# Score products over all 128 rows and two head slots' P·V on both column halves, in a hybrid attention and mixture-of-experts block

## The chip, the cores and the metric

The kernel runs on one core of a Trainium2 chip. Its time is the device time of one execution in microseconds (us). In the listings PE is the tensor engine (matrix products), PEld its loading of the stationary operand, DVE the vector engine, ACT the scalar engine, POOL the general engine, SP the engine whose queue issues nearly all DMA transfers. Engines run side by side, each takes its instructions in their order, and semaphores make one wait for another. SBUF is the on-chip memory with 128 rows (partitions); PSUM holds the products' sums.

## What is computed

One decoder layer over 256 tokens of width 1024, in float32:

```
h = rmsnorm(x);  proj = h @ w_in
y_dil = dilated attention: 3 groups x 8 heads (dilation 1, 4, 16), head width 64;
        the 3 heads of a slot are combined by their softmax denominators
y_swa = sliding-window attention: 16 query heads, 2 key/value heads, with sinks
x += (sigmoid(gate_d) * (y_dil @ w_br_dil) + sigmoid(gate_s) * (y_swa @ w_br_swa)) @ w_out
x += experts: one group of 4, then 2 of its 8 SwiGLU experts per token, width 512
out = rmsnorm(x)
```

All 32 experts' weights are read: each has 6 MB, against 36 MB of dense weights.

## The kernel before

**Stages.** The dense weights come as tiles of 512 columns by 4 row blocks (1 MB, class `Stream`, four slots). `convert` (L232) splits each pair of row blocks on ACT (L248) and DVE (L249) into two float32r parts, high and low. A dense product of two split operands is three matmuls (`three`, L345): high·high, low·high, high·low, each 128x128 by 128x256 or 128x512; they are called `acc` in the trace. The units of 512 columns follow one another: q, k and v of the dilated heads; then k, v, q of the windowed heads and the first gate, with the eight dilated head slots (`dil_slot`, L558) interleaved step by step (L773); then the second gate and the first branch product, interleaved with the eight pairs of windowed heads (`swa_pair`, L521; L780); then the branch and output products, the router, and the 32 experts one after the other (L1061 on).

**Scores.** The score products are split in three as well. For the head of slot i = 2a + b, tile `qa[:, b, a]` holds the high parts of q on 64 rows and its low parts on the other 64, and `ka[:, b, a]` holds the high parts of k on both halves of the rows. So one product over 128 rows gives high·high + low·high (L565). The third, high·low, runs over only the 64 rows with the high parts of q, against `kal`, the low parts of k (L566). Four small float32 products per half of the queries (L570) add the two wider groups. Windowed heads do the same with `kx` and `kxl` (L528, L529), 256 keys for either half of the queries. A plain float32 product shows as two matmul instructions in the trace, a float32r one as one.

**After the scores**, `softmax` (L487) runs on DVE and ACT, PE transposes the probabilities (`dtp` L579, `stp` L542), and P·V follows (`dpv`, `spv`). In `dil_slot` the slot with b = 0 writes the columns of the array that give PSUM rows 0 to 63, the one with b = 1 those of rows 64 to 127, each slot in its own step (L586 to L590). In `swa_pair` both heads' products of one size stand next to each other, on either half of the columns (L546 to L551). The two `pT` buffers of the transposed probabilities are in tile `turnedp` (L519).

**Order and memory.** `pipelined` (L596) takes the scores of one slot, the transposes of the one before and the values of the one before that; `interleave` (L616) puts these steps between those of the dense units at a ratio. The framework's scheduler then fixes each engine's order. SBUF is handed out in numbered slots of 1 MB. Expert weights come in 1 MB pieces (`ew`; two DMAs of 512 KB for gate and up, or one for down) into a ring of such slots. Slots 20 and 23 are in the ring from the start (L639), and two pieces are loaded during the first units (L769 to L771); each `release` (L661) adds slots that have become free and issues one piece for each. The ring's later pieces are issued as an expert's products free their slots.

Of the kernel before, what the change touches and what calls it, by code (L numbers as in the profile page):

```python
# [17 lines left out]
P = 128  # L18
T = 256
# [18 lines left out]
def _constants():  # L38
    """Tables that depend on the shapes alone: distances of the score blocks with the
    masked ones far away, unit and triangular matrices, counters, the scales of q."""  # L40
# [44 lines left out]
def tile_hybrid_block(  # L85
# [24 lines left out]
    # x and the output come with the tokens by their class, the token modulo 4, and in order within it:  # L110
    # place 64 c + j is token 4 j + c.
# [19 lines left out]
    # ---------------------------------------------------------------- loads  # L131
# [22 lines left out]
    class Stream:  # L154
        """Dense weights, 512 columns by 4 row blocks of 128, in the order they are used."""
# [71 lines left out]
    # ---------------------------------------------------------------- splitting of dense weights  # L227
# [4 lines left out]
    def convert(order=lambda i: i):  # L232
        """Split the next two row blocks of a dense weight into two float32r parts, exactly."""
# [35 lines left out]
    # ---------------------------------------------------------------- h = rmsnorm(x), transposed, split  # L269
# [52 lines left out]
    # ---------------------------------------------------------------- dense products  # L322
    # q and k of the widest products in two float32r parts: on one half of the partitions the high parts of
    # a head's q, on the other its low parts; the high parts of k on both; the low parts of k.
    qa = slot(4, [P, 2, 4, T], "qa", F32R)
    ka = slot(22, [P, 2, 4, T], "ka", F32R)
    s21 = slot(21, [P, 2048], "ks", F32R)
    kal = s21[:, 0:1024].rearrange("p (a t) -> p a t", a=4)
    kx, kxl = (s21[:, c:c + 512].rearrange("p (j t) -> p j t", j=2) for c in (1024, 1536))
# [31 lines left out]
    def evac(un, half, o):  # L361
# [41 lines left out]
        elif kind == "kd" and arg == 0:  # L403
            c = slice(2 * half, 2 * half + 2)
            for b in range(2):
                own = slice(64 * b, 64 * b + 64)
                for r in (own, slice(64 - 64 * b, 128 - 64 * b)):
                    A.copy(ka[r, b, c, :], ov[own])
                V.tensor_tensor(out=kal[own, c, :], in0=ov[own], in1=ka[own, b, c, :].bitcast(F32), op=ALU.subtract)
# [11 lines left out]
        elif kind == "brs":  # L421
            if half == 0:
                # the first half of the sum is in two parts before the second half begins, which takes its place
                mixed[arg] = (sb.tile([P, 2, 4, T], F32R, tag="PT", name="mixed0") if arg == 0
                              else slot(0, [P, 2, 4, T], "mixed1", F32R))
# [14 lines left out]
    def unit_steps(u):  # L440
        """One unit as steps of a row-block pair each: two passes over the same weights."""
# [44 lines left out]
    # ---------------------------------------------------------------- attention  # L486
    def softmax(pt_, parts, sinkcols=None):  # L487
        """parts: (scores in PSUM, distances, scale, start of the minimum) -> P and 1/denominator.
        Scores come with the sign turned, so their minimum is minus the maximum."""
# [29 lines left out]
    turnedp = sb.tile([P, 2, 768], F32, tag="PT", name="pT")  # L519

    def swa_pair(a):  # L521
        kv = a // 4
        sc = quad[2 * (a % 2):2 * (a % 2) + 2]
        for b in range(2):
            r = slice(64 * b, 64 * b + 64)
            for t in range(NT):
                q, o = qs[b][:, a, t * P:(t + 1) * P], sc[b][:, T * t:T * t + T]
                mm(o, q, kx[:, kv, :], True, False)  # L528
                mm(o, q[r], kxl[r, kv, :], False, True)  # L529
# [28 lines left out]
    def dil_slot(i):  # L558
        """One head slot of the dilated attention: in the two wider groups a query's keys are of its class."""
# [3 lines left out]
        for h in range(2):  # L563
            q = qa[:, b, a, h * P:(h + 1) * P]
            mm(sc[h][:, 0:T], q, ka[:, b, a, :], True, False)  # L565
            mm(sc[h][:, 0:T], q[r], kal[r, a, :], False, True)  # L566
# [8 lines left out]
        pT = turnedp[:, i % 2, :]  # L575
# [6 lines left out]
        if b == 0:  # L582
            late["dpv"] = bank("V", [P, 512], f"dpv{a}")
        o = late["dpv"]
        hc = slice(64 * i, 64 * i + 64)
        for t in range(NT):  # L586
            mm(o[r, 0:T], vd[t][:, 0, hc], pT[:, T * t:T * t + T], t == 0, False)
        for c in range(4):
            mm(o[r, 64 * c:64 * c + 64], vd[c // 2][:, 1 + c % 2, hc], pT[:, 2 * T + 64 * c:2 * T + 64 * c + 64],
               False, c == 3)  # L590
        if b == 1:
            A.copy(yd[:, 0, a, :], o[:, 0:T])
            V.tensor_tensor(out=yd[:, 1, a, :], in0=o[:, 0:T], in1=yd[:, 0, a, :].bitcast(F32), op=ALU.subtract)
        yield

    def pipelined(gens, parts):  # L596
        """Scores of one, transposes of the one before, values of the one before that."""
# [34 lines left out]
    # ---------------------------------------------------------------- expert weights  # L632
# [6 lines left out]
    ring = [20, 23]  # L639
# [21 lines left out]
    def release(*slots):  # L661
        """These slots are free for expert weights from here on."""
# [14 lines left out]
    # ---------------------------------------------------------------- routing  # L677
# [12 lines left out]
    def route_piece(t, k):  # L690
        """256 columns of x2 of one token tile: squares summed, transposed for the logits."""
# [23 lines left out]
    def route_pick(t):  # L715
        """The first of the best groups, its two best experts, the pairs' places in line."""
# [411 lines left out]
```

## Time and profile before

| | us |
|---|---|
| device time, median of 3 runs (780.91 to 783.07) | 781.64 |
| span of the profiled execution, first to last instruction | 779.8 |
| PE busy in the span | 674.3 |
| DVE busy | 294.6 |
| ACT busy | 225.9 |
| bytes moved by DMA | 249.89 MB |

The execution's own time is not listed apart from its span; the median of the timed runs is 1.84 us above the span. PE is busy in all of the first half and less in the second, where the DMA moves a steady 408 GB/s. A share of busy time over the whole span hides that the stages have different limits, so the stages are read one by one below.

### The profile page before, as it was taken

How to read it: one execution, taken by the hardware profiler on the slowest of the kernel's cores; microseconds unless marked ns; L12 is line 12 of the kernel's file. 1: busy time of each engine (PE TensorE's matmuls, PEld its weight loads, DVE VectorE, ACT ScalarE, POOL GpSimd, SP SyncE). 2: the span in 40 equal slices, each digit the busy share in tenths (PEclk: the TensorE clock that was granted, in tenths of full speed). 3: DMA queues.
4: the chain of work that ended last, by engine and by line, in shares of the span. 5: the costliest groups of instructions: out<-in, count | busy, mean ns of one | idle time of the engine just before them, and what ended most of it. 6: DMA issues, size and time to landing. Idle time of an engine off the chain costs nothing.

```text
span 779.8 us, 15115 instructions
## 1 busy us (share of the span) xinstructions
PE 674.3 (86%) x6417; PEld 478.2 (61%) x6417; DVE 294.6 (38%) x749; ACT 225.9 (29%) x448; POOL 2.1 (0%) x10
## 2 busy tenths in 40 slices
PE   9999999999999999999987777878787787767682
PEld 8998988889788998765645334444434344433341
DVE  6564667874666675632222111211211111111102
ACT  5444575755677454310101000100000000000003
POOL 0000000000000000000000000000000000000000
PEclk9999999999999999999999679888978958987787
DMA  8786554336634778999999999999999999999993
GB/s 310 248 307 207 162 187 139 109 109 254 232 109 156 273 293 311 337 369 407 408 408 410 408 408 408 408 407 408 409 409 408 409 409 409 408 407 409 408 408 135
DMA packets 81054, 249.89 MB, mean 320 GB/s; under 512 B 8652, under 2 KB 10072, under 8 KB 80984
## 3 DMA queue, kind: packets, MB, share of 16 engines
q1 hardware_dynamic: 80824, 248.82, 83.5%
q8 instruction: 52, 0.85, 0.4%
q14 instruction: 18, 0.15, 0.1%
q10 hardware_dynamic: 160, 0.07, 0.0%
HBM read 247.82 MB, written 1.05 MB: 319 GB/s over the span
## 4 chain that ended last, share of the span: by engine, by line
PE 55%; DMA 38%; DVE 3%; ACT 2%; issue 1%; SPq 0%; ACTq 0%; DVEq 0%
PE acc L121 29%; DMA ew<-in_w_e_up_dram 17%; DMA ew<-in_w_e_down_dram 11%; DMA ew<-in_w_e_gate_dram 10%; PE gu L121 7%; PE quad L121 7%; PE dn L121 4%; PE ga L121 3%; PE dpv L121 1%; PE ct L899 1%; PE spv L121 1%; PE dtp L579 1%; PE stp L542 1%; PE ct L121 1%; PE atp L127 1%
## 5 line engine op out<-in xcount | busy, mean ns | idle before, releaser
L121 PE MATMUL gu<-ew,xes 128*32 128x256 f32 x2048 | 153.7, 416 | 36.9 <-DMA ew<-in_w_e_up_dram 36.9
L121 PE MATMUL acc<-hT_hi,wh 128*128 128x256 f32 x800 | 147.7, 285 | 0.8 <-DVE qa L401 0.8
L121 PEld LDWEIGHTS acc<-hT_hi,wh 128*128 128x128 f32 x800 | 122.0, 188 | 4.4 <-issue 1.5
L121 PEld LDWEIGHTS gu<-ew,xes 128*32 128x32 f32 x2048 | 64.9, 116 | 93.8 <-issue 64.0
L249 DVE TENSOR_TENSOR wh<-w,wh 128x1024 fp32r<-128x1024 f32 (+1 forms) x84 | 100.2, 1198 | 44.3 <-ACT wh L248 42.7
L121 PE MATMUL acc<-hT_lo,wh 128*128 128x256 f32 x400 | 111.4, 279 | 0.0
L248 ACT CAST wh<-w 128x1024 fp32r<-128x1024 f32 (+1 forms) x84 | 86.1, 1028 | 49.7 <-PE acc L121 42.9
L121 PE MATMUL dn<-ew,ws 128*32 128x256 f32 x1024 | 84.8, 468 | 3.5 <-DMA ew<-in_w_e_down_dram 2.8
L925 DVE TENSOR_TENSOR ws<-ws,gu 128x128 f32<-128x128 f32 x32 | 9.2, 286 | 194.0 <-ACT ws L922 194.0
L121 PEld LDWEIGHTS acc<-hT_lo,wh 128*128 128x128 f32 x400 | 75.1, 188 | 0.4 <-issue 0.4
L922 ACT ACTIVATE ws<-gu 128x128 f32<-128x128 f32 x32 | 8.9, 278 | 215.1 <-PE gu L121 215.1
L121 PEld LDWEIGHTS dn<-ew,ws 128*32 128x32 f32 x1024 | 33.1, 128 | 33.2 <-issue 12.8
L951 ACT ACTIVATE y_hi<-dn,gsl 128x256 fp32r<-128x256 f32 x32 | 15.2, 474 | 114.5 <-PE dn L121 114.5
L121 PE MATMUL ga<-ws,x_again 128*128 128x128 f32 x256 | 39.3, 315 | 4.8 <-DVE ws L938 3.8
L121 PEld LDWEIGHTS ga<-ws,x_again 128*128 128x128 f32 x256 | 36.0, 221 | 8.9 <-DVE ws L938 6.9
L953 DVE SCALAR_TENSOR_TENSOR y_lo<-dn,gsl,y_hi 128x256 fp32r<-128x256 f32 x32 | 15.5, 483 | 66.6 <-ACT y_hi L951 66.6
L121 PE MATMUL quad<-y_hi,cts 32*128 32x256 f32 x256 | 24.0, 361 | 15.0 <-ACT y_hi L951 15.0
L121 PEld LDWEIGHTS quad<-y_hi,cts 32*128 32x128 f32 x256 | 14.2, 208 | 33.3 <-ACT y_hi L951 32.1
L121 PE MATMUL quad<-y_lo,cts 32*128 32x256 f32 x256 | 32.6, 392 | 2.3
L860 ACT ACTIVATE xes<-ga,fcol 128x128 f32<-128x128 f32 x32 | 11.7, 368 | 79.0 <-DVE xes L862 79.0
L892 DVE TENSOR_SCALAR ws<-cs,pos 128x128 f32<-128x128 f32 x64 | 17.8, 281 | 41.6 <-PE ct L121 41.6
L121 PEld LDWEIGHTS quad<-y_lo,cts 32*128 32x128 f32 x256 | 19.0, 205 | 21.9 <-issue 14.3
(199 smaller groups left out, 769.0 us busy)
## 6 DMA issues: line engine op xcount, KB each, us to landing
ew<-in_w_e_gate_dram SPq DMA_DIRECT2D x128, 512.0 KB, 12.7
ew<-in_w_e_up_dram SPq DMA_DIRECT2D x128, 512.0 KB, 12.8
ew<-in_w_e_down_dram SPq DMA_DIRECT2D x63, 1024.0 KB, 12.7
w<-in_w_in_dram SPq DMA_DIRECT2D x29, 1024.0 KB, 5.2
w<-in_w_br_swa_dram SPq DMA_DIRECT2D x4, 1024.0 KB, 5.2
w<-in_w_out_dram SPq DMA_DIRECT2D x4, 1024.0 KB, 6.6
w<-in_w_in_dram SPq DMA_DIRECT2D x4, 512.0 KB, 5.8
w<-in_w_br_dil_dram SPq DMA_DIRECT2D x2, 1024.0 KB, 5.2
```

Source lines behind the costliest of these rows:

```text
L121: i = PE.matmul(o, lhsT, rhs, start=start, stop=stop, skip_group_check=True)
L127: i = PE.transpose(o, src, ident)
L248: order(A.copy(w[:, 0, :, :ncol], r))
L249: order(V.tensor_tensor(out=w[:, 1, :, :ncol], in0=r, in1=w[:, 0, :, :ncol].bitcast(F32), op=ALU.subtract))
L542: PE.transpose(tp[:, j * P:(j + 1) * P], pp[:, 384 * b + j * P:384 * b + (j + 1) * P], ident)
L579: PE.transpose(tp[:, h * P:(h + 1) * P], pp[:, 384 * h + j * P:384 * h + (j + 1) * P], ident)
L860: A.activation(dst, src, AF.Copy, scale=col)
L892: eq = V.tensor_scalar(dd[:, t, :].rearrange("p (g s) -> p g s", g=REP), cs[:, C_CNT:C_CNT + CAP].unsqueeze(1).to_broadcast([P, REP, CAP]) ...
L922: A.activation(ac, gu[:, 0:P], AF.Silu)
L925: V.tensor_tensor(out=ac, in0=ac, in1=gu[:, P:2 * P], op=ALU.mult)
L951: A.activation(y_hi, dn[:, 0:256], AF.Copy, scale=gsl)
L953: V.scalar_tensor_tensor(out=y_lo, in0=dn[:, 0:256], scalar=gsl, in1=y_hi.bitcast(F32), op0=ALU.mult, op1=ALU.subtract)
```

## The change

It has four parts. (1) `kal` gets a slot of its own and holds the low parts of k on both halves of the rows; the third score product of `dil_slot` and of `swa_pair` uses all 128 rows of q. In the product of q's low half with the low parts of k, low·low is added, which the version before left out. (2) In `dil_slot` the four wide score products come first, then all eight small ones; in `swa_pair` the first half of the queries gets only the 128 keys that it uses. (3) P·V of two dilated slots is done in one step, product by product alternating between the two column halves; `pT` has four buffers, two of them in slot 20. (4) Slots 20 and 23 come into the ring only after the dilated slots, so the two early pieces are no longer loaded ahead; the steps' ratio goes from 40 to 36.

```diff
-    kal = s21[:, 0:1024].rearrange("p (a t) -> p a t", a=4)
-    kx, kxl = (s21[:, c:c + 512].rearrange("p (j t) -> p j t", j=2) for c in (1024, 1536))
+    kal = slot(23, [P, 2, 4, T], "kal", F32R)
+    kx, kxl = (s21[:, c:c + 512].rearrange("p (j t) -> p j t", j=2) for c in (0, 512))
...
-                for r in (own, slice(64 - 64 * b, 128 - 64 * b)):
+                both = (own, slice(64 - 64 * b, 128 - 64 * b))
+                for r in both:
                     A.copy(ka[r, b, c, :], ov[own])
-                V.tensor_tensor(out=kal[own, c, :], in0=ov[own], in1=ka[own, b, c, :].bitcast(F32), op=ALU.subtract)
+                for r in both:
+                    V.tensor_tensor(out=kal[r, b, c, :], in0=ov[own], in1=ka[own, b, c, :].bitcast(F32),
+                                    op=ALU.subtract)
...
     turnedp = sb.tile([P, 2, 768], F32, tag="PT", name="pT")
+    more = slot(20, [P, 2048], "pT2")[:, 0:1536].rearrange("p (i c) -> p i c", i=2)
+    turned4 = [turnedp[:, 0, :], turnedp[:, 1, :], more[:, 0, :], more[:, 1, :]]
...
-                q, o = qs[b][:, a, t * P:(t + 1) * P], sc[b][:, T * t:T * t + T]
-                mm(o, q, kx[:, kv, :], True, False)
-                mm(o, q[r], kxl[r, kv, :], False, True)
+                n = P * (t + 1)
+                q, o = qs[b][:, a, t * P:(t + 1) * P], sc[b][:, T * t:T * t + n]
+                mm(o, q, kx[:, kv, 0:n], True, False)
+                mm(o, q, kxl[:, kv, 0:n], False, True)
...
             mm(sc[h][:, 0:T], q, ka[:, b, a, :], True, False)
-            mm(sc[h][:, 0:T], q[r], kal[r, a, :], False, True)
+            mm(sc[h][:, 0:T], q, kal[:, b, a, :], False, True)
+        for h in range(2):
             for g in (1, 2):
...
-        pT = turnedp[:, i % 2, :]
+        pT = turned4[i % 4]
...
         if b == 0:
-            late["dpv"] = bank("V", [P, 512], f"dpv{a}")
-        o = late["dpv"]
-        hc = slice(64 * i, 64 * i + 64)
+            return
+        o = bank("V", [P, 512], f"dpv{a}")
+        two = [(slice(64 * j, 64 * j + 64), slice(64 * (2 * a + j), 64 * (2 * a + j) + 64), turned4[(2 * a + j) % 4])
+               for j in range(2)]
         for t in range(NT):
-            mm(o[r, 0:T], vd[t][:, 0, hc], pT[:, T * t:T * t + T], t == 0, False)
+            for r, hc, pT in two:
+                mm(o[r, 0:T], vd[t][:, 0, hc], pT[:, T * t:T * t + T], t == 0, False)
         for c in range(4):
-            mm(o[r, 64 * c:64 * c + 64], vd[c // 2][:, 1 + c % 2, hc], pT[:, 2 * T + 64 * c:2 * T + 64 * c + 64],
-               False, c == 3)
...
+            cl = slice(64 * c, 64 * c + 64)
+            for r, hc, pT in two:
+                mm(o[r, cl], vd[c // 2][:, 1 + c % 2, hc], pT[:, 2 * T + 64 * c:2 * T + 64 * c + 64], False, c == 3)
...
-    ring = [20, 23]
+    ring = []
...
-    for i, _ in enumerate(steps_of(("qd", "kd", "vd"))):
-        if i % 12 == 11 and i > 20 and nchunk[0] < len(ring):
-            prefetch(1)
+    for _ in steps_of(("qd", "kd", "vd")):
+        pass
...
-    interleave(steps_of(("kvs", "qs", "gd")), pipelined((dil_slot(i) for i in range(8)), 3), 40.0 / 34.0)
-    release(7, 8, 9, 22, 6)
+    interleave(steps_of(("kvs", "qs", "gd")), pipelined((dil_slot(i) for i in range(8)), 3), 36.0 / 34.0)
+    release(20, 23, 7, 8, 9, 22, 6)
```

PE's order around the scores of one dilated slot, before (`quad` is the scores' bank, `ks` the tile that held the low parts of k, `qk` the small operands of the two wider groups; the row of 64x64 stands for two products):

```order
L121 MATMUL quad0_61<-ka_196,qa_195 128x256
L121 MATMUL quad0_61<-ks_197,qa_195 128x256
L121 MATMUL quad0_61<-qk1_198 64x64 x2
L121 MATMUL quad0_61<-qk2_199 64x64 x2
L121 MATMUL quad1_62<-ka_196,qa_195 128x256
L121 MATMUL quad1_62<-ks_197,qa_195 128x256
L121 MATMUL quad1_62<-qk1_198 64x64 x2
L121 MATMUL quad1_62<-qk2_199 64x64 x2
```

and with the change:

```order
L121 MATMUL quad0_61<-ka_196,qa_195 128x256
L121 MATMUL quad0_61<-kal_197,qa_195 128x256
L121 MATMUL quad1_62<-ka_196,qa_195 128x256
L121 MATMUL quad1_62<-kal_197,qa_195 128x256
L121 MATMUL quad0_61<-qk1_199 64x64 x2
L121 MATMUL quad0_61<-qk2_200 64x64 x2
L121 MATMUL quad1_62<-qk1_199 64x64 x2
L121 MATMUL quad1_62<-qk2_200 64x64 x2
```

The four wide products now stand together; between 128-row and 64-row operands PE changes twice in a slot, where it changed six times.

PE's order at the scores of the first windowed pair and the dense products behind them, before (in a row x4 stands for the two halves of the queries, each with a 128-row product and a 64-row one in turn):

```order
L121 MATMUL quad_61<-ks,qs_203 128x256 x4
L121 MATMUL quad_62<-ks,qs_204 128x256 x4
L121 MATMUL acc_2068<-hT_hi,wh_1_2000 128x256 x2
L121 MATMUL acc_2068<-hT_lo,wh_1_2000 128x256
L121 MATMUL acc_2068<-hT_hi,wh_1_2000 128x256 x2
```

and with the change:

```order
L121 MATMUL quad_61<-ks,qs_204 128x128 x2
L121 MATMUL quad_61<-ks,qs_204 128x256 x2
L121 MATMUL quad_62<-ks,qs_205 128x128 x2
L121 MATMUL quad_62<-ks,qs_205 128x256 x2
L121 MATMUL acc_2074<-hT_hi,wh_1_1993 128x256 x2
L121 MATMUL acc_2074<-hT_lo,wh_1_1993 128x256
```

Eight products stay eight, all over 128 rows, four of them with half the columns.

PE's order at P·V of slots 2 and 3, before (of slot 2; the four rows of slot 3 read the same, and stand some 45 rows further down):

```order
L121 MATMUL acc_1495<-hT_hi,wh_3_1478 128x256 x2
L121 MATMUL acc_1495<-hT_lo,wh_3_1478 128x256
L121 MATMUL dpv_1581<-pT,v_200 64x256
L121 MATMUL dpv_1581<-pT,v_201 64x256
L121 MATMUL dpv_1581<-pT,v_200 64x64 x2
L121 MATMUL dpv_1581<-pT,v_201 64x64 x2
```

and with the change (both slots):

```order
L121 MATMUL dpv1_1687<-pT2_210,v0_201 64x256 x2
L121 MATMUL dpv1_1687<-pT2_210,v1_202 64x256 x2
L121 MATMUL dpv1_1687<-pT2_210,v0_201 64x64 x4
L121 MATMUL dpv1_1687<-pT2_210,v1_202 64x64 x4
```

The products of the two slots alternate; what stood in eight blocks of six products stands in four blocks of twelve.

## Rows read from the trace of the kernel before

**Rows 1.** The page: its span, and the GB/s of its 40 slices.

```profile
span 779.8 us, 15115 instructions
...
GB/s 310 248 307 207 162 187 139 109 109 254 232 109 156 273 293 311 337 369 407 408 408 410 408 408 408 408 407 408 409 409 408 409 409 409 408 407 409 408 408 135
```

**Rows 2.** Busy times by stretches: start and end, length, engines' busy us, clock, DMA share, GB/s.

```profile
133.00:153.00 20.00, 20.00 (x175) 17.64 (x175) 16.95 (x34) 14.61 (x27) 0.00 (x0) 1.00 0.33 107
...
213.00:233.00 20.00, 20.00 (x142) 16.24 (x141) 14.49 (x50) 15.13 (x38) 0.00 (x0) 1.00 0.32 101
...
267.00:322.00 55.00, 54.06 (x360) 49.31 (x358) 35.67 (x81) 21.27 (x38) 1.83 (x4) 1.00 0.83 308
181.00:245.00 64.00, 64.00 (x460) 53.76 (x459) 39.98 (x125) 39.85 (x95) 0.00 (x0) 1.00 0.52 182
245.00:331.00 86.00, 84.51 (x637) 73.05 (x636) 56.11 (x147) 41.44 (x83) 1.83 (x4) 1.00 0.83 308
343.00:765.00 422.00, 333.83 (x3806) 183.09 (x3806) 73.21 (x257) 33.61 (x88) 0.00 (x0) 0.86 1.02 407
```

**Rows 3.** The same view, the whole stretch of interleaved attention.

```profile
113.00:267.00 154.00, 152.75 (x1194) 129.45 (x1193) 106.21 (x270) 98.88 (x203) 0.00 (x0) 1.00 0.50 172
```

**Rows 4.** SP's waits from 281 to 345 us: total us, times, longest.

```profile
SPq L646 <- PE gu L121: 10.9, 3, 9.0
...
SPq L653 <- PE dn L121: 6.2, 1, 6.2
```

**Rows 5.** PE's waits from 320 us to the end.

```profile
PE gu L121 <- DMA ew<-in_w_e_up_dram: 36.9, 35, 2.8
```

**Rows 6.** Chain of waits: start, us until the next piece, what; in and behind a dilated slot.

```profile
135.18 1.42 PE acc L121 x12
136.60 1.81 PE quad L121 x20
138.41 1.56 PE acc L121 x12
139.97 0.22 PE dtp L579 x2
...
141.60 1.47 PE dpv L121 x12
```

**Rows 7.** The same view, a windowed pair.

```profile
228.14 2.30 PE quad L121 x8
230.44 1.58 PE acc L121 x12
232.35 0.80 PE spv L121 x8
```

**Rows 8.** PE in order of time, scores of the first dilated slot (start, us to the last end).

```profile
113.28 0.28 PE L121 MATMUL quad<-ka,qa 128*128 128x256 f32 x1
113.49 0.38 PE L121 MATMUL quad<-ks,qa 64*128 64x256 f32 x1
113.80 0.45 PE L121 MATMUL quad<-qk 64*64 64x64 f32 x8
114.18 0.38 PE L121 MATMUL quad<-ka,qa 128*128 128x256 f32 x1
```

**Rows 9.** The same view, an expert's products on four column quarters in turn.

```profile
395.74 2.80 PE L121 MATMUL gu<-ew,xes 128*32 128x256 f32 x48
```

**Rows 10.** DVE in order of time, low parts of k and the last split of the next unit.

```profile
102.70 0.69 DVE L409 TENSOR_TENSOR ks<-acc,ka 64x512 fp32r<-64x512 f32 x1
103.53 1.23 DVE L249 TENSOR_TENSOR wh<-w,wh 128x1024 fp32r<-128x1024 f32 x1
```

**Rows 11.** PE in order of time: the first products that read that split.

```profile
104.80 0.62 PE L121 MATMUL acc<-wh,hT_hi 128*128 128x512 f32 x2
```

**Rows 12.** DVE's waits from 100 to 270 us: total us, times, longest.

```profile
DVE wh L249 <- ACT wh L248: 19.2, 15, 3.5
```

**Rows 13.** DMA issues: KB each, us to landing.

```profile
ew<-in_w_e_gate_dram SPq DMA_DIRECT2D x128, 512.0 KB, 12.7
```

More of the change, by code (lines that the diff above doesn't have):

```diff
@@ L524, in swa_pair @@
         for b in range(2):
-            r = slice(64 * b, 64 * b + 64)
             for t in range(NT):
-                q, o = qs[b][:, a, t * P:(t + 1) * P], sc[b][:, T * t:T * t + T]
-                mm(o, q, kx[:, kv, :], True, False)
-                mm(o, q[r], kxl[r, kv, :], False, True)
+                n = P * (t + 1)
+                q, o = qs[b][:, a, t * P:(t + 1) * P], sc[b][:, T * t:T * t + n]
+                mm(o, q, kx[:, kv, 0:n], True, False)
+                mm(o, q, kxl[:, kv, 0:n], False, True)
         pp = pps[:, a % 2, :]
@@ L582, in dil_slot @@
         if b == 0:
-            late["dpv"] = bank("V", [P, 512], f"dpv{a}")
-        o = late["dpv"]
-        hc = slice(64 * i, 64 * i + 64)
+            return
+        o = bank("V", [P, 512], f"dpv{a}")
+        two = [(slice(64 * j, 64 * j + 64), slice(64 * (2 * a + j), 64 * (2 * a + j) + 64), turned4[(2 * a + j) % 4])
+               for j in range(2)]
         for t in range(NT):
-            mm(o[r, 0:T], vd[t][:, 0, hc], pT[:, T * t:T * t + T], t == 0, False)
+            for r, hc, pT in two:
+                mm(o[r, 0:T], vd[t][:, 0, hc], pT[:, T * t:T * t + T], t == 0, False)
         for c in range(4):
-            mm(o[r, 64 * c:64 * c + 64], vd[c // 2][:, 1 + c % 2, hc], pT[:, 2 * T + 64 * c:2 * T + 64 * c + 64],
-               False, c == 3)
-        if b == 1:
-            A.copy(yd[:, 0, a, :], o[:, 0:T])
-            V.tensor_tensor(out=yd[:, 1, a, :], in0=o[:, 0:T], in1=yd[:, 0, a, :].bitcast(F32), op=ALU.subtract)
+            cl = slice(64 * c, 64 * c + 64)
+            for r, hc, pT in two:
+                mm(o[r, cl], vd[c // 2][:, 1 + c % 2, hc], pT[:, 2 * T + 64 * c:2 * T + 64 * c + 64], False, c == 3)
+        A.copy(yd[:, 0, a, :], o[:, 0:T])
+        V.tensor_tensor(out=yd[:, 1, a, :], in0=o[:, 0:T], in1=yd[:, 0, a, :].bitcast(F32), op=ALU.subtract)
         yield
```

## The prediction

> **What bounds the kernel now.** I read the page first, then busy times by stretches, the waits of SP and PE, and last the chain of waits and PE in order of time. The slices of the page [rows 1] show two kernels in one: up to the sixteenth slice the DMA moves 100 to 340 GB/s with gaps, from the nineteenth on a flat 408. The stretches say what rules each. From 113 to 267 us, where both attentions are interleaved with dense products, PE is busy 152.75 of 154 us, DVE 106.2 and ACT 98.9 [rows 3]. From 267 to 322 us (branch and output products, router) PE has 54.06 of 55. From 343 to 765 us PE has idle time and the DMA share is 1.02 [rows 2]; there PE waits 36.9 us for expert weights [rows 5]. So PE rules up to the first experts and the DMA from about 343 us on.
>
> What joins the two decides whether time saved before 267 us reaches the end. Just before the DMA becomes steady, SP's queue stands still for want of free slots: it waits 10.9 us for gate-up products and 6.2 us for a down product of the first experts [rows 4]. The ring is full then, and PE's progress alone frees it. If PE comes there earlier, the steady phase, with the same bytes to move from there, begins and ends earlier by as much. This needs a DMA that has caught up by then, and it had room: its share is 0.52 from 181 to 245 us and 0.83 from 245 to 331 us [rows 2], which leaves 0.48·64 + 0.17·86 = 45.3 us idle.
>
> **The change, part by part.** Each price is PE time between 113 and 267 us, at a granted clock of 1.00, the higher of the two levels.
>
> *Windowed scores.* Twelve `acc` products of 128x256 take 1.42 us, 0.118 each [rows 6]. The eight score products of a pair take 2.30, and the twelve `acc` behind them 1.58 instead of 1.42 [rows 7]: 2.46 us. The difference is not in the columns, which are as many per product; it goes with the change between operands of 128 and of 64 rows. In the dilated slot the starts show it: 0.21 us from the full product to the half one, 0.31 from there to the small ones [rows 8]. With the change all eight are full, between full neighbours. At 0.118 each they take 0.94 us, a saving of 1.52 per pair and 12.1 us in eight pairs. Four of them have only 128 columns, for which no row of a split product stands here; a transpose of 128 columns takes 0.11 [rows 6], so I take 0.118 and no further gain. The bounds: at half of 0.118 the saving is 14.0 us; at today's mean of 0.29 for those four it is 6.6 us.
>
> Here a rule speaks against the change. The rows have a full product and a half one at 0.29 us each in alternation, and full ones at 0.118 among themselves. The Trainium skill ("TensorE: Matmul & The Clock Gate", section "Why this matters for your kernels") says that one product over 32 rows takes the same time as over 128 and that the gain lies in tiles running at once. By that, filling the rows would win nothing, and two half products on the two halves of the rows would be the better use. The rule holds for one product; the rows show the price of the alternation, and I go by the rows. What is left of the rule is the third rival.
>
> *Dilated scores.* A slot takes 1.81 us, and the twelve `acc` behind it 1.56 instead of 1.42 [rows 6]: 1.95 in all, with six changes of operand shape. Four full products at 0.118 are 0.47. The small ones take 0.38 per eight, from their start to the next full one [rows 8], with the change behind them in it. After: 0.47, the late start of the first small one (0.31 - 0.118 = 0.19), 0.76, and 0.14 behind: 1.56, a saving of 0.39. If each of the four changes that go costs that 0.19, the saving is 0.76. I take 0.55, between them, 4.4 us for eight slots, with bounds of 3.1 and 6.1.
>
> *P·V of two slots at once.* One slot takes 1.47 us for twelve instructions [rows 6] with 4·256 + 8·64 = 1536 columns. The windowed P·V has the same 1536 columns, in four of 256 and four of 128, but on both column halves in turn, and takes 0.80 [rows 7]. At its rate a pair of dilated slots takes 1.60 instead of 2.94: 1.34 saved, 5.4 us in four pairs. That alternating columns cost no change of the kind above is shown by the experts' products: 48 of 256 columns, over four quarters in turn, in 2.80 us, 0.058 each [rows 9]. Bounds: 0 if the halves ran in series, 5.9 if they overlapped wholly.
>
> *Low parts of k twice.* Four more subtractions of 0.69 us on DVE, before 113 us. There the last split of the next unit ends at 103.53 + 1.23 = 104.76 [rows 10], and the products that read it start at 104.80 [rows 11], so there is no cover. Three of the added subtractions stand ahead of it, 2.1 us; how much of that DVE's gaps further ahead take up, none of these rows says. I take 1.0 us lost, between 0 and 2.1.
>
> *The two early pieces.* 4 transfers of 512 KB [rows 13], 2.1 MB, 5.1 us at 408 GB/s, leave the first units and come after the dilated slots. Cost zero: the idle time of the DMA from 181 to 245 us, 30.7 us, hides them. If that were gone they would cost 5.1 us. In SP's queue the piece for the slot of `ka` now stands ahead of dense tiles that are needed only in the second gate's products; it waits for the last dilated scores. The four `pT` buffers and the steps' ratio cost nothing by themselves: PE's list has no fewer dense products between scores and transposes.
>
> The sum on PE: 12.1 + 4.4 + 5.4 = 21.9 us. Then 152.75 falls to 130.9 us, while DVE keeps 106.2 of work, and 17.4 of waits for ACT's half of the weight splits (19.2 from 100 to 270 us [rows 12], by 154/170): 123.6, or 94% of PE. In single stretches it is tight already: 16.95 of 20 us on DVE, 15.13 of 20 on ACT [rows 2]. So some of the saving comes back as waits of PE for scores' and transposes' copies. No row prices that; between nothing and half I take 15%, 3.3 us, since the two chains are of nearly one length but the pipeline gives a slot a whole step of slack. What is late next is DVE.
>
> 21.9 - 1.0 - 3.3 = 17.6 us off the span: 779.8 - 17.6 = 762.2. The runs' median lies 1.84 above the span, so **764.0 us**.
>
> **The rivals.**
> *DVE and ACT become the bound.* For it: the 94% above, and stretches where they are nearly full. Against: PE hardly waits for either now. If half of the saving goes, 21.9/2 - 1.0 = 9.9, the time is 771.7.
> *The DMA decides, and it is slower.* For it: 2.1 MB more behind the dilated slots, in a time that shrinks by 17 us; were the DMA busy without a gap from the dilated slots on, PE's gain would be worth nothing and the pieces would add 5.1 us: 786.8. It decides from where 17.6 + 5.1 = 22.7 us exceed the idle time up to the full ring. Against: that is 45.3 us, of which 14.6 lie behind 245 us, where all is triggered by PE and moves along.
> *Full rows win nothing.* The change does not do what it says: the wide pairs keep 0.29 and 0.31 us per product because the price lies in something else than the row count (the same q loaded twice, say). Then only P·V saves: 5.4 - 1.0 - 0.4 = 4.0, 777.6 us. The skill's rule above would have it so. Against: in [rows 8] the first full product after `acc` is followed at once, and the delays stand at each change of shape.
>
> **How the numbers follow.** Forecast 0.65, DVE and ACT 0.20, full rows without effect 0.08, DMA 0.03, and 0.04 for what I don't see. The forecast's own ends are 14.0 + 6.1 + 5.9 = 26.0 with next to no waits, at most 24 off (758), and 6.6 + 3.1 + 5.4 less 1.0 and 2, some 12 (770). The second rival's 771.7 needs a margin of 2. So the range is 758 to 774. Less than 0.3% (2.3 us) can hardly be told from no change. All but the DMA and the unseen are faster by more: 0.93 faster, 0.03 within, 0.04 slower.
>
> **What would show it.** Eight windowed scores near 0.95 us without a longer `acc` run behind; a dilated slot near 1.4 us in one block; P·V of a pair near 1.6 us; the first expert's products some 17 us earlier; the steady 408 GB/s beginning some 17 us earlier, with the same bytes left; new waits of PE for copies, 3 to 4 us in all. I am wrong if the alternation on the column halves is as dear as that on the rows, if PE's waits grow beyond 8 us, or if the DMA has no gap between the dilated slots and the first expert.

## The result, and the profile after

| | us (median, lowest to highest) | ratio to before, 95% interval |
|---|---|---|
| before | 781.54 (780.91 to 783.07) | |
| changed | 760.07 (759.4 to 760.18) | 0.9721 [0.9707, 0.9735] |

The changed kernel is 21.5 us faster. Forecast were 764.0 us, between 758 and 774: the sign was right, and the time lies within the range, with 3.9 us more gained than forecast.

The page of the changed kernel, its span and the GB/s of its 40 slices (before: [rows 1]):

```profile
span 758.4 us, 15111 instructions
...
GB/s 317 234 217 223 146 136 219 113 112 279 336 116 360 342 281 295 334 410 408 408 409 408 409 409 409 407 408 410 408 408 409 409 408 409 409 408 402 408 409 139
```

Where the time came from is read at one landmark, the first product of the first expert. Before, PE in order of operations, the group of the experts' gate-up products up to 330 us (count, then min/median/max in ns, then first and last start):

```profile
L121 PE MATMUL gu<-ew,xes x82: 379/379/403, 324.6 to 329.9; 128*32 128x256 f32 x82
```

The same group after the change:

```profile
L121 PE MATMUL gu<-ew,xes x192: 378/379/404, 304.2 to 330.0; 128*32 128x256 f32 x192
```

It starts 324.6 - 304.2 = 20.4 us earlier. From there to the end of the span are 779.8 - 324.6 = 455.2 us before and 758.4 - 304.2 = 454.2 after. So 20.4 of the 21.4 us of span were won before the experts. The last 1.0 is no more than this stretch varies by: in a second profile of the changed kernel (e12 below) it takes 759.1 - 303.8 = 455.3 us.

Busy times by stretches after the change (columns as in [rows 2]):

```profile
113.00:247.00 134.00, 130.08 (x1207) 120.38 (x1206) 105.78 (x272) 98.87 (x205) 0.00 (x0) 1.00 0.62 219
...
224.00:310.00 86.00, 83.86 (x654) 74.72 (x657) 58.68 (x155) 43.14 (x89) 1.82 (x4) 1.00 0.84 308
322.00:744.00 422.00, 330.39 (x3815) 181.29 (x3807) 73.22 (x258) 33.54 (x88) 0.00 (x0) 0.87 1.02 407
```

The first is the stretch of the interleaved attention, 20 us shorter than in [rows 3] for the same work of DVE (105.78 against 106.21) and ACT. PE has 130.08 us in it, the 152.75 of before less 22.7. The granted clock is 1.00 in both, the higher level. The last row is the steady stretch of the DMA, moved by 21 us, with the same share and rate as before [rows 2].

PE in order of time in the kernel before, at P·V of one dilated slot and at the scores of another (start, us to the last end, count; the first pair of sizes is rows and columns of the stationary operand, here called its shape):

```profile
141.32 0.28 PE L121 MATMUL acc<-hT_lo,wh 128*128 128x256 f32 x1
141.53 1.54 PE L121 MATMUL dpv<-pT,v 128*64 128x256 f32 x12
143.00 0.50 PE L121 MATMUL acc<-hT_hi,wh 128*128 128x256 f32 x2
143.34 0.28 PE L121 MATMUL acc<-hT_lo,wh 128*128 128x256 f32 x1
...
157.59 0.28 PE L121 MATMUL quad<-ka,qa 128*128 128x256 f32 x1
...
159.50 0.50 PE L121 MATMUL acc<-hT_hi,wh 128*128 128x256 f32 x2
```

The same view of the changed kernel, at a dilated slot's scores, at P·V of two slots and at a windowed pair's scores:

```profile
134.46 0.28 PE L121 MATMUL quad<-ka,qa 128*128 128x256 f32 x1
134.57 0.28 PE L121 MATMUL quad<-kal,qa 128*128 128x256 f32 x1
...
134.81 0.28 PE L121 MATMUL quad<-kal,qa 128*128 128x256 f32 x1
135.02 0.68 PE L121 MATMUL quad<-qk 64*64 64x64 f32 x16
135.63 0.50 PE L121 MATMUL acc<-hT_hi,wh 128*128 128x256 f32 x2
135.97 0.28 PE L121 MATMUL acc<-hT_lo,wh 128*128 128x256 f32 x1
...
138.84 1.55 PE L121 MATMUL dpv<-pT,v 128*64 128x256 f32 x24
...
206.04 1.08 PE L121 MATMUL quad<-ks,qs 128*128 128x128 f32 x8
206.96 0.40 PE L121 MATMUL acc<-hT_hi,wh 128*128 128x256 f32 x2
207.20 0.28 PE L121 MATMUL acc<-hT_lo,wh 128*128 128x256 f32 x1
```

The four wide products now start 0.11 to 0.12 apart. From the first of them to the dense product behind the slot are 135.63 - 134.46 = 1.17 us. The two `acc` after it take 135.97 - 135.63 = 0.34 until the third, where undisturbed ones take 207.20 - 206.96 = 0.24, so a slot costs 1.17 + 0.10 = 1.27. Before, read in the same view, it cost 159.50 - 157.59 = 1.91 us and the same 0.10 behind (two `acc` in 0.50 to their last end instead of 0.40), 2.01 in all. P·V of two slots takes 1.55 to its last end, where one slot alone took 1.54. The eight windowed products take 206.96 - 206.04 = 0.92, and the `acc` behind them are not late, against 2.46 before.

What was given back stands in PE's waits, from 95 to 300 us. Before:

```profile
PE dtp L579 <- DVE pT L357: 1.0, 1, 1.0
PE vsT L380 <- DVE vT L377: 0.2, 1, 0.2
```

After (total us, times, longest):

```profile
PE stp L548 <- DVE pps L517: 1.2, 2, 0.7
PE vsT L381 <- DVE vT L378: 1.1, 1, 1.1
PE acc L121 <- DVE qs L402: 0.7, 1, 0.7
PE dtp L586 <- ACT pT L360: 0.7, 2, 0.5
...
PE acc L121 <- DVE kal L412: 0.2, 1, 0.2
PE dtp L586 <- DVE pT L358: 0.2, 1, 0.2
```

The row left out is a wait of 0.3 us in the router, which before stood behind 300 us. The six shown make 4.1 us, against 1.2 before: 2.9 us given back. The list counts idle time from the modelled end of the product before, so a delay can be longer than its wait; for `kal` it is (see the part on the low parts of k).

SP's waits for free slots are still there, from 259 to 325 us:

```profile
SPq L656 <- PE gu L121: 10.1, 2, 9.0
...
SPq L663 <- PE dn L121: 7.4, 1, 7.4
```

They answer to the 10.9 and 6.2 us of [rows 4]: the ring is full in front of the first experts as before, and PE frees it, only earlier.

### The profile page after: what moved, and what is told of

Read it like the earlier page. It is cut to its first block, busy times and chain, and to the rows that moved or that the text cites. A ratio compares the mean times of both kernels' runs of the same rounds, so it can differ in the third digit from the quotient of the medians.

```text
span 758.4 us, 15111 instructions
## 1 busy us (share of the span) xinstructions
PE 646.1 (85%) x6417; PEld 465.5 (61%) x6417; DVE 295.8 (39%) x753; ACT 224.4 (30%) x448; POOL 2.1 (0%) x10
## 5 line engine op out<-in xcount | busy, mean ns | idle before, releaser
L121 PE MATMUL acc<-hT_hi,wh 128*128 128x256 f32 x800 | 145.9, 284 | 1.4 <-DVE qa L402 0.8
L121 PE MATMUL dn<-ew,ws 128*32 128x256 f32 x1024 | 81.4, 451 | 4.6 <-DMA ew<-in_w_e_down_dram 4.0
L121 PEld LDWEIGHTS dn<-ew,ws 128*32 128x32 f32 x1024 | 32.1, 125 | 33.9 <-issue 10.9
L121 PE MATMUL acc<-wh,hT_hi 128*128 128x512 f32 x96 | 30.9, 397 | 0.3 <-DVE kal L412 0.2
```

Source lines behind the costliest of these rows:

```text
L121: i = PE.matmul(o, lhsT, rhs, start=start, stop=stop, skip_group_check=True)
```

## The experiments

Twelve runs were made. In each the start of the first expert's product in the trace lies 455.2 to 457.4 us ahead of the median time, so differences of more than about 2 us arise ahead of the experts. Gains and losses are counted against the changed kernel's 760.07 us, or against the kernel before as it was timed next to the run (781.08 for e1 to e4, 780.99 for e9).

| kernel | median us | ratio to before, 95% interval | first `gu` at |
|---|---|---|---|
| e1, before without early pieces | 781.14 | 1.0001 [0.9991, 1.001] | 325.3 |
| e2, windowed scores alone | 769.84 | 0.9857 [0.9841, 0.9874] | 313.6 |
| e3, only their columns cut | 779.36 | 0.9978 [0.9968, 0.9987] | 324.2 |
| e4, half products in one block | 771.24 | 0.9871 [0.9854, 0.9887] | 315.0 |
| e9, half products by two | 774.37 | 0.9907 [0.9892, 0.9922] | 317.4 |
| e6, changed, dilated third product on 64 rows | 763.25 | 0.9772 [0.9757, 0.9788] | 306.8 |
| e10, changed, small products apart | 761.61 | 0.9748 [0.9733, 0.9763] | 305.9 |
| e5, changed, P·V in series | 763.05 | 0.9762 [0.9747, 0.9777] | 307.2 |
| e8, changed, second `kal` by POOL | 760.22 | 0.9728 [0.9713, 0.9743] | 302.8 |
| e7, changed, 256 keys | 758.23 | 0.9699 [0.9686, 0.9712] | 302.3 |
| e11, e7 and e8 together | 758.42 | 0.9707 [0.9692, 0.9721] | 301.7 |
| e12, changed, again | 760.02 | 0.9727 [0.9713, 0.974] | 303.8 |

**Do the early pieces matter (e1)?** The kernel before, with the later entry of slots 20 and 23 from the fourth part of the change and nothing else of it (the steps' ratio stays 40, and no run tests 36 alone):

```diff
-    ring = [20, 23]
+    ring = []
...
-        if i % 12 == 11 and i > 20 and nchunk[0] < len(ring):
-            prefetch(1)
+        pass
...
-    release(7, 8, 9, 22, 6)
+    release(20, 23, 7, 8, 9, 22, 6)
```

> The kernel before without the two early expert pieces: slots 20 and 23 join the ring only after the dilated slots. Theory (the DMA has idle time that hides them, PE sets the start of the steady phase): 781.5 us, within 1 us of before, and the first expert's products at 324 to 325 us as before. Rival (the DMA decides from the dilated slots on): 5.1 us slower, about 786.7.

781.14 us against 781.08, no difference, and the first expert's products at 325.3: the 2.1 MB that come later cost nothing in the kernel before. In the changed one the DMA's share from 224 to 310 us is 0.84 (above), where the stretch that answers to it had 0.83 [rows 2], so it has room there too. The rival in which the DMA decides falls.

**The windowed scores alone (e2).** The kernel before with the change's `swa_pair`:

```diff
-            r = slice(64 * b, 64 * b + 64)
...
-                mm(o, q, kx[:, kv, :], True, False)
-                mm(o, q[r], kxl[r, kv, :], False, True)
+                mm(o, q, kx[:, kv, 0:n], True, False)
+                mm(o, q, kxl[:, kv, 0:n], False, True)
```

> The kernel before with the change to the windowed scores alone (128 rows, and 128 keys for the first half of the queries). Theory: the eight products of a pair take about 0.9 us instead of 2.3, the acc run behind them 1.42 instead of 1.58; 12 us less PE work, 1 to 2 given back to waits: about 771 us. Rival (full rows win nothing): 780 to 781.5 us.

769.84 us, 11.2 less than before and more than half of the whole gain, from four lines. Either the full rows or the columns that were cut with them won this; the next run separates the two.

**Rows or columns (e3)?** As e2, but the third product keeps its 64 rows; only the keys that the first half of the queries doesn't use are cut.

```diff
-                mm(o, q, kx[:, kv, :], True, False)
-                mm(o, q[r], kxl[r, kv, :], False, True)
+                mm(o, q, kx[:, kv, 0:n], True, False)
+                mm(o, q[r], kxl[r, kv, 0:n], False, True)
```

> The kernel before with only the columns cut: the first half of the queries gets 128 keys, the third product stays on 64 rows, full and half products alternate. Theory (the price is the change between 128-row and 64-row operands): the eight products stay above 2.0 us, total 779.8 to 781.5. Rival (the columns made the gain): the eight fall to 1.2 to 1.5 us, total 772 to 774.

779.36 us, 1.7 less than before and a little below the range expected. PE in order of time in that kernel:

```profile
205.53 2.24 PE L121 MATMUL quad<-ks,qs 128*128 128x128 f32 x8
207.69 0.50 PE L121 MATMUL acc<-hT_hi,wh 128*128 128x256 f32 x2
```

The eight still take 207.69 - 205.53 = 2.16 us, and the `acc` behind them are still late (0.50 for two). A quarter of the columns is gone, and less than a tenth of the time: columns don't hold the 2.30. By the difference, some 9.5 of e2's 11.2 us are the full rows', and the rival in which they win nothing falls.

**Is the price the half product or the change to it (e4)?** The kernel before, with all four full products of a pair first and then the four half ones, the two heads (opposite halves of the rows) in turn. Its score sums do not all hold the three products; the instructions and their sizes are those of before.

```diff
+        for t in range(NT):
+            for b in range(2):
+                r = slice(64 * b, 64 * b + 64)
+                q, o = qs[b][:, a, t * P:(t + 1) * P], sc[b][:, T * t:T * t + T]
                 mm(o, q[r], kxl[r, kv, :], False, True)
```

> The kernel before with the windowed scores in another order only: the four 128-row products first, then the four 64-row ones, alternating between the two halves of the rows; same rows and columns as before. Theory (each change of shape costs about 0.19 us, and there are two instead of eight): 0.47 + 0.19 + 0.47 + 0.16 = 1.29 us per pair with what is behind it, instead of 2.46, 9.4 us less PE work, about 773 us; if the half products on opposite rows run at once, 1.06 us and about 771. Rival (a product over 64 rows is dear by itself, about 0.46 us): 2.3 us, no gain, 781.5.

```profile
222.77 1.07 PE L121 MATMUL quad<-ks,qs 128*128 128x256 f32 x8
223.77 0.50 PE L121 MATMUL acc<-hT_hi,wh 128*128 128x256 f32 x2
...
223.33 0.39 PE L121 MATMUL quad<-ks,qs 64*128 64x256 f32 x2
```

771.24 us: the same eight products as before, in another order, win 10 us. The rows above are PE in order of time of e4. The first two have all eight in 1.00 us and 0.10 behind (0.50 instead of 0.40). The last, from a window of its own (223.41 to 223.50 us), has two half products on opposite halves of the rows done in 0.39 us together, where a single one takes 0.38 in [rows 8]: they start within 0.01 us of each other and run at once. That both products of a sum go into one place of PSUM is not the price either: in the changed kernel `ka` and `kal` do so 0.11 us apart.

**Two in a row (e9).** Full, full, half, half for either half of the queries, so four changes in a pair where before had eight and e4 two:

```diff
-        for b in range(2):
-            r = slice(64 * b, 64 * b + 64)
-            for t in range(NT):
+        for t in range(NT):
+            for b in range(2):
...
+            for b in range(2):
+                r = slice(64 * b, 64 * b + 64)
+                q, o = qs[b][:, a, t * P:(t + 1) * P], sc[b][:, T * t:T * t + T]
                 mm(o, q[r], kxl[r, kv, :], False, True)
```

> The kernel before, with each windowed pair's scores in the order full, full, half, half for the first half of the queries and again for the second: eight products as before, the same 64-row third product, but four changes between 128-row and 64-row operands instead of eight, and the two half products next to each other on opposite halves of the rows. Theory (the change of shape costs about 0.2 us each and two half products on opposite row halves run at once, as the grouped run showed with two changes and 1.00 + 0.11 us per pair): 4 x 0.118 + 2 x 0.118 + 4 x 0.2 = 1.5 us per pair with what follows, against 2.46 before; 0.95 saved, 7.6 us in eight pairs, so about 773.5 us. Rival A (a half product is dear by itself, and the grouped run won only by having all four in a row): near 781. Rival B (changes cost, but half products don't overlap): 0.94 + 0.8 = 1.74 per pair, 5.8 us saved, 775.5.

PE in order of time of e9:

```profile
216.88 1.46 PE L121 MATMUL quad<-ks,qs 128*128 128x256 f32 x8
218.27 0.51 PE L121 MATMUL acc<-hT_hi,wh 128*128 128x256 f32 x2
```

1.39 and 0.11 behind (0.51 instead of 0.40): 1.50 us per pair, the 1.5 of the theory and not the 1.74 of rival B. The time, 774.37, lies between the two, but the first expert's product comes 324.6 - 317.4 = 7.2 us earlier, where the theory has 7.6 and rival B 5.8. With eight products at 0.118 or, where two half ones run at once, four and two, and c for a change:

| kernel | changes | us per pair | c if half products overlap | c if they don't |
|---|---|---|---|---|
| before | 8 | 2.46 | 0.19 (none adjacent) | 0.19 |
| e9 | 4 | 1.50 | 0.20 | 0.14 |
| e4 | 2 | 1.10 | 0.20 | 0.08 |

One price fits all three only if the half products overlap, as e4's row shows them to do: 0.2 us on average for each change between 128-row and 64-row operands. It comes in two parts. In e4 the four full products would be through at 222.77 + 4 x 0.118 = 223.24, and the first half product starts at 223.33, 0.09 late; what follows the first product behind a change is late again by about 0.1, as the 0.50 of two `acc` at 223.77 shows.

**The dilated third product back on 64 rows (e6)**, in the changed kernel:

```diff
-            mm(sc[h][:, 0:T], q, kal[:, b, a, :], False, True)
+            mm(sc[h][:, 0:T], q[r], kal[r, b, a, :], False, True)
```

> The changed kernel with the third dilated score product back on 64 rows; the small products still stand together behind the wide ones. Theory (changes of shape at 0.19 us; five in a slot instead of two): 0.6 us more per slot, 4.6 us in eight, about 764.5 us. Rival (most of the gain in the dilated slot comes from putting the small products together): 761 or less.

PE in order of time of e6:

```profile
135.66 0.28 PE L121 MATMUL quad<-ka,qa 128*128 128x256 f32 x1
...
137.42 0.50 PE L121 MATMUL acc<-hT_hi,wh 128*128 128x256 f32 x2
```

137.42 - 135.66 = 1.76 us against 1.17, or 0.59 in eight slots 4.7 us. The time, 763.25 us, grew by 3.2 only: with slower scores the waits for `qs` and for ACT's `pT` (0.7 each) are gone from PE's list, and that for `vT` fell from 1.1 to 0.4, so 2.1 us of the 4.7 come back, and the first expert's product is 306.8 - 304.2 = 2.6 us later.

**The small products apart (e10)**, in the changed kernel: the line `for h in range(2):` ahead of the small products goes, so each half's four stand behind its two wide ones.

> The changed kernel, with the four small score products of each half of the queries put back behind that half's two wide products: four changes of operand shape in a dilated slot instead of two; the third product stays over 128 rows. Theory (the changes are the price): two changes more per slot at 0.19 each, 0.38 us, 3.0 us in eight slots, less what PE waited anyway: 762 to 763. Rival (full rows are the whole gain in the dilated slots, the order of the small ones is worth nothing): 760.

761.61 us, 1.6 more than e12 and a little less than expected. PE in order of time of e10:

```profile
135.07 0.28 PE L121 MATMUL quad<-ka,qa 128*128 128x256 f32 x1
...
136.59 0.51 PE L121 MATMUL acc<-hT_hi,wh 128*128 128x256 f32 x2
```

136.59 - 135.07 = 1.52 us against 1.17: two changes more, 0.35 us, the theory's price. In eight slots that is 2.8 us, of which 1.6 reached the end. Full rows and fewer changes are one and the same gain, in two pieces.

**P·V one slot after the other (e5)**, in the changed kernel:

```diff
-        for t in range(NT):
-            for r, hc, pT in two:
+        for r, hc, pT in two:
+            for t in range(NT):
...
-        for c in range(4):
-            cl = slice(64 * c, 64 * c + 64)
-            for r, hc, pT in two:
+            for c in range(4):
+                cl = slice(64 * c, 64 * c + 64)
```

> The changed kernel with P.V of the two dilated slots in one step but one slot after the other, not alternating between the column halves. Theory (only alternating lets the halves run at once): 24 instructions in about 2.9 us instead of 1.55, 5.4 us more PE work, about 765 us. Rival (the order inside the step does not matter, or the gain came from the four buffers and the fewer steps): 1.6 us and 760.

763.05 us, 3.0 more. PE in order of time of e5:

```profile
156.66 2.69 PE L121 MATMUL dpv<-pT,v 128*64 128x256 f32 x24
...
156.66 0.43 PE L121 MATMUL dpv<-pT,v 128*64 128x256 f32 x1
```

The second row is the first product alone (window 156.87 to 156.90 us). In the changed kernel the first two, one on either half of the columns, are done in nearly the same time (window 139.0 to 139.1 us):

```profile
138.84 0.44 PE L121 MATMUL dpv<-pT,v 128*64 128x256 f32 x2
```

So the two column halves run at once where they alternate, and the 24 instructions take 1.55 instead of 2.69. That is 1.14 per pair, 4.6 us in four, less waits that went with it: the 0.7 for `qs` is gone, and that for ACT's `pT` fell from 0.7 to 0.2. So 4.6 - 1.2 = 3.4 of PE's time was lost, and 3.0 showed.

**The second `kal` by POOL (e8)**, in the changed kernel:

```diff
-                for r in both:
-                    V.tensor_tensor(out=kal[r, b, c, :], in0=ov[own], in1=ka[own, b, c, :].bitcast(F32),
-                                    op=ALU.subtract)
+                V.tensor_tensor(out=kal[own, b, c, :], in0=ov[own], in1=ka[own, b, c, :].bitcast(F32),
+                                op=ALU.subtract)
+                nc.gpsimd.tensor_copy(kal[both[1], b, c, :], kal[own, b, c, :].bitcast(F32))
```

> The changed kernel with the second copy of the low parts of k made by POOL from the first instead of by DVE. Theory (the added subtractions delay a weight split on DVE by about 0.6 us of PE time): 759.5 us, 0.5 faster than the changed kernel. Rival (the delay is hidden further on): 760.1, no difference; if POOL's copies come too late for the first dilated scores, 761 to 763.

760.22 us (758.92 to 761.27), no gain over the changed kernel. But the five runs spread over 2.3 us, in which 0.5 can't be seen, and the trace, of a run of 759.07, does show a gain on PE: the two delays that the four added subtractions cause (shown further down) are not in it, and the first expert's product starts at 302.8, 1.0 us before e12's. Whether that reaches the end stays open.

**256 keys for both halves (e7, e11, e12).** In the changed kernel `n = P * (t + 1)` becomes `n = T`, so PE has more columns to do:

> The changed kernel with 256 keys for both halves of the queries in the windowed scores, all over 128 rows. Theory (a product of 128 columns costs hardly less than one of 256): the eight take 0.94 to 0.97 us instead of 0.9, at most 0.6 us in all, 760 to 760.7 us. Rival (columns count in full): 0.053 us for each of 32 products, 1.7 us, 761.8.

758.23 us (757.62 to 759.01), faster than the changed kernel, where 0 to 0.6 more was expected. It was run again with e8's edit beside the changed kernel itself:

> The changed kernel with 256 keys for both halves of the queries (the faster of the variants so far) and with the second copy of the low parts of k made by POOL. Theory: the copy's place is worth nothing that can be measured, so the time is that of the 256-key version, 758.2 within 0.7. Rival: the POOL copy frees DVE before the dilated slots and about 0.5 us of it reaches the end once the waits at the first windowed pair are gone: 757.5.

> The changed kernel itself, without any edit, in the same job as the 256-key version with POOL: what the 256-key versions gain is read against this. Theory (256 keys move the first pair's transposes behind more dense products, which is real): 760.1 here, 1.5 to 2 us above the 256-key version of this job. Rival (the difference was one of chips or jobs): within 0.7 us of it.

758.42 us (757.01 to 759.2) and 760.02 (759.79 to 760.84): the difference of 1.6 us is there again, and POOL's copy adds nothing that the medians show. PE in order of time in the changed kernel, first windowed pair:

```profile
194.24 1.08 PE L121 MATMUL quad<-ks,qs 128*128 128x128 f32 x8
...
197.44 0.30 PE L548 MATMUL stp<-cs,pps 128*128 128x128 f32 x1 [0.51 <-DVE pps L517]
```

The same place in e7:

```profile
193.82 1.11 PE L121 MATMUL quad<-ks,qs 128*128 128x256 f32 x8
...
197.18 0.27 PE L548 MATMUL stp<-cs,pps 128*128 128x128 f32 x1
```

The cut columns were worth 0.03 us per pair. But with them the scheduler put 14 dense products between the scores and the transposes that need their softmax, and with 256 keys 21. In the first case PE waits 0.51 us, in the second not at all; at the last pair it waits 0.66 or not. Other traces bear it out: the kernel before and the other runs with 256 keys have 21 dense products there, while e3, which has only the 128 keys of the change, and e2, which has these and the full rows, have 14. With fast scores (e2) 1.2 us of waits for `pps` come with that, with slow ones (e3) none. That these 1.2 us make up most of the 1.6 is what the traces say; an experiment that moves the transposes alone was not made.

## Why the prediction was right, point by point

**What bounds the kernel: right.** PE's time ahead of the experts reaches the end nearly one to one (20.4 us at the landmark, 21.4 in the span), SP's waits for the full ring stay, and the steady stretch moves as a block. e1 shows that of the 45.3 us of room read from [rows 2] at least the 5.1 that the two pieces need were there. (The sum for the rival in which the DMA decides is 781.64 + 5.1 = 786.7, not 786.8; nothing hangs on it.)

**Windowed scores: right.** Forecast 12.1 us; 2.46 - 0.92 = 1.54 per pair, 12.3 in eight. e2 has 11.2 at the end, with 1.2 of waits for `pps` already in it. The bound of 0.29 for products with 128 columns was unneeded.

**Dilated scores: right in kind, mis-sized.** 2.01 - 1.27 = 0.74 per slot, 5.9 us, where 0.55 and 4.4 stood; the upper bound was 6.1. The failing step is the one that put the slot at 1.56 and then met it halfway. The small products were taken at 0.38 per eight with a change behind them, twice; sixteen in a row have one change behind them and take 0.61, not 0.76. The first of them is late by 0.21 - 0.12 = 0.09, not by 0.19: that figure was the step from 64x256 to the small ones. This step also tells that rows alone are not what counts. Of the six changes in a slot before, which the section on the change counts as all between 128-row and 64-row operands, only four are; two lead from the 64-row product to the small ones, which have 64 rows too, but 64 columns instead of 128 in the stationary operand.

**P·V: right.** Forecast 5.4. A slot of 1.47 [rows 6] showed 1.54 to its last end in the order of time; two now show 1.55, so about 1.48, and 2 x 1.47 - 1.48 = 1.46 per pair or 5.8 us. Alternating column halves overlapped nearly wholly, at the upper bound.

**Low parts of k: the size right by luck, one reading wrong.** Forecast 1.0 us. PE and DVE in order of time in the changed kernel, at the end of the unit ahead:

```profile
105.31 0.62 PE L121 MATMUL acc<-wh,hT_hi 128*128 128x512 f32 x2
105.76 0.40 PE L121 MATMUL acc<-wh,hT_lo 128*128 128x512 f32 x1
106.29 0.74 PE L121 MATMUL acc<-wh,hT_hi 128*128 128x512 f32 x2
...
107.32 0.28 PE L121 MATMUL quad<-ka,qa 128*128 128x256 f32 x1
107.81 0.47 PE L121 MATMUL acc<-wh,hT_hi 128*128 128x512 f32 x1 [0.20 <-DVE kal L412]
...
105.01 1.23 DVE L249 TENSOR_TENSOR wh<-w,wh 128x1024 fp32r<-128x1024 f32 x1
```

Products of this kind start 0.23 us apart (two in 105.76 - 105.31 = 0.45). The step to 106.29 takes 0.53: the split, which began at 103.53 before, ends at 106.24. The step from 107.32 to 107.81, behind a product of 0.12, takes 0.49: PE waits for the last added subtraction. That is 0.30 + 0.37, and with 0.12 and 0.07 in the products just behind (0.74 instead of 0.62, 0.47 instead of 0.40) about 0.9 us; the list of waits has only 0.2 of it. In e8 both delays are gone. The size was luck, since 1.0 was chosen between 0 and 2.1 without a row. And there was some cover, against the reading of [rows 10] and [rows 11]: the products that answer to those at 104.80, counted from the start of the unit, start here at 105.31, while the split is still running, so those that need it come only three products later.

**Waits given back: right in size, one premise wrong.** Forecast 3.3, measured 2.9, or 2.7 without the 0.2 for `kal`, and of the forecast kind, PE waiting for copies and softmax of DVE and ACT. But the premise that PE's list has no fewer dense products between scores and transposes does not hold for the windowed pairs: at the first it is 14 instead of 21, at the last 12 instead of 19, and the 1.2 us of waits for `pps` stand just there (e7). The DVE and ACT rival did not come: DVE has 105.78 us of 134. e5, e6 and e10 show the same waits from the other side: in sum they shrink when PE is slower (in e10, though, one of 1.3 us for DVE's `pT` is new), and so each part undone costs 1.2 to 1.6 us less at the end than on PE.

The sum from the traces is 12.3 + 5.9 + 5.8 - 2.7 - 0.9 = 20.4 us, the 20.4 of the landmark, though the parts are known to some tenths only. Of the 3.9 us that the forecast missed, 2.1 are the three savings (24.0 instead of 21.9) and 0.7 the two losses (3.6 instead of 4.3); the rest is about the 1.0 us behind the landmark.

**Full rows against half products.** Grouped half products (e4) show that two products on opposite halves of the rows do run at once. The Trainium skill ("TensorE: Matmul & The Clock Gate", section "Why this matters for your kernels") says that for products over few rows the gain lies in such concurrency, and e4's 1.00 us for four full and four half products agrees. Both ways were open here, then, and what decides between them is the changes: full rows have none and take 0.92 us, grouped halves have two and take 1.10. The rival that took the rule as a reason against full rows failed since it left out the change.

## What to carry to other kernels

Look at the starts of neighbouring matrix products whose stationary operands differ in shape: here each change between 128 and 64 rows cost 0.2 us, more than the product itself (0.118), so fill the rows (with a harmless term if need be) or put products of one shape together before cutting columns. Products on opposite halves of columns or rows run at once when they alternate. After PE has become faster, look at how many dense products still stand between a score and the transpose that waits for its softmax: fewer columns made this kernel 1.6 us slower.

## What the hardware showed that was not expected

- The change of shape is a price by itself, near 0.2 us, and hardly depends on the moving columns: with a quarter of them cut, the eight products still took 2.16 us (e3).
- It is not bound to the rows. At P·V of the kernel before all operands have 128 rows, and only the stationary columns go from 128 to 64 and back: the first product starts 141.53 - 141.32 = 0.21 us after the `acc` ahead of it instead of 0.12, and the third `acc` behind follows the first after 143.34 - 143.00 = 0.34 instead of 0.24. P·V and the small products are also in plain float32, so no run tells what the change of number type adds there; the windowed scores (e2 to e4, e9) are float32r throughout.
- Half products in turn on opposite halves of the rows run two at a time: in e4 two of them took 0.39 us together and all eight products 1.00. In the kernel before it was their full neighbours that made each cost 0.29.
- Alternating between column halves has no such price: 24 instructions, each on 64 columns of the array, took 1.55 us in turn and 2.69 one half after the other (e5).
